# Causal masks added by VectorE in the instruction that finds the maximum, and the second gate's sums in the second layer

## The chip, the cores and the metric

The kernel runs on one core of one Trainium2 chip. Its engines work side by side: TensorE (PE in the profile, its weight loads PEld) multiplies, VectorE (DVE) and ScalarE (ACT) work element by element, GpSimd (POOL) prepares constants, SyncE (SP) issues most DMAs. The metric is the device time of one execution in microseconds; a lower time is better.

## The reference

Two layers work on x, 256 rows of 1024 numbers. Each normalises x, scales and shifts it by sums over `ada_w` (adaLN), mixes the rows by attention, and adds the result times a gate, which is another sum over `ada_w`. Layer 1 mixes with three attentions (compressed, selected and window keys), layer 2 with one; both have 16 heads of 64 that share 4 key heads. With 256 rows every window and every selection covers all earlier rows, so each score matrix has the same mask: a row sees the keys up to its own place.

```python
for i in range(DEPTH):
    shift, scale, gate = jnp.split(cond @ ada_w[i] + ada_b[i], 3, axis=-1)
    h = rms_norm(x, norm_g[i]) * (1 + scale[:, None, :]) + shift[:, None, :]
    ...
    x = x + gate[:, None, :] * y

def masked_softmax(s, mask):
    s = jnp.where(mask, s.astype(jnp.float32), -jnp.inf)
    m = jnp.max(s, axis=-1, keepdims=True)
    e = jnp.exp(s - jnp.where(jnp.isfinite(m), m, 0.0))
    return e / jnp.maximum(jnp.sum(e, axis=-1, keepdims=True), 1e-30)

p = masked_softmax(s_own, m_own).astype(v.dtype)
return jnp.einsum('bcgrk,bkgd->bcgrd', p, v_own)
...
return (o * jax.nn.silu(z)) @ w_out
```

## The kernel before

**The order of the work.** The program doesn't issue an instruction where the code calls it. `T`, `A`, `V`, `G`, `Q` record calls for TensorE, ScalarE, VectorE, GpSimd and SyncE in one `Plan`; at the end `plan.issue()` writes the order of each engine. It keeps a clock per engine, takes the cost of an instruction from `_cost`, the buffers of a tile from its tag, and among the operations that are ready the one that can start first, at equal times by a level: `URGENT`, `CHAIN`, `FILL`. So an operation recorded at `FILL` goes into gaps of the plan. All instructions carry line 373, the place in `issue()` that emits them; this document tells them apart by the names of their tiles. `_cost` gives a VectorE instruction 1.042 ns for each element and 68 ns (the line with `fast`), whether or not it also writes an accumulator.

**The products with weights.** A weight piece is 128 rows of 1024 numbers (512 KB), loaded by SP into `raw` (5 buffers). ScalarE rounds it into `hi` (4), VectorE subtracts, `lo = raw - hi` (4), and TensorE makes three products: hi with the high part of h, lo with the high part, hi with the low part. `chunk` does this for queries and keys; `z_blocks(w, c0, zT)` for the transposed z, in products of 256 columns at level `FILL`, into the two PSUM buffers `acc`; `out_products` for the output, with the transposed, gated heads in `qg`.

**The attention.** `make_q` normalises and rotates queries on VectorE (`ss`, `rs`, `n_out`, `rot`, `n_parts`), and TensorE transposes them. `scores` makes one PSUM tile `ps` for two heads: four products of 256 columns, and one more product of the identity in bf16 (`identB`) with a mask of 0 and a large negative number (`tri`, from `tri2`), which adds the mask. Then `top` finds the negative maximum of each row on VectorE (TENSOR_REDUCE into `tiny`), `exps` takes the exponential on ScalarE from PSUM into `p` (6 buffers) with the maximum as bias, and adds up the row. VectorE inverts the sums and scales `p`, TensorE transposes `p` (`ps<-identF,p`), ScalarE copies to `pT`, TensorE multiplies with the values (`ps<-pT,VA`), and VectorE multiplies with z (`g<-zT,ps`, then `qg<-g,qg`).

- `compressed(hf)`, twice in layer 1: scores of eight heads against 16 compressed keys, one mask product from `maskC` ahead of them, softmax in the tile `pc`, then its transposes (`ps<-identF,pc`).
- `pair_a(i)`, eight times in layer 1: three score groups for two heads (selected and window keys for the first 128 rows in one, then one each for the second 128 rows).
- `pair_b(i)`, eight times in layer 2: two score groups, 128 and 256 keys.

**Work in the background.** `side` is a list of generators, and `beside()` takes one step of the first of them. In layer 1 `beside()` is called between the pairs and the z pieces. The list holds the compression's products (`cmp_steps`), the first layer's gate (`ada_gate(0)`), and for the second layer two halves of scale and shift (`ada_ss`) with `ada_gate(1)` between them. `ada_gate(1)` loads eight pieces of `ada_w` into `raw` and sums them on VectorE, one SCALAR_TENSOR_TENSOR of 1024 elements each at level `FILL`; then two products with ones (`ps<-gate,ones`) spread the sum over the partitions. `x_update` of layer 2 needs that gate, behind the output products.

Of the kernel before, what the change touches and what calls it, by code (L numbers as in the profile page):

```python
# [9 lines left out]
F32 = mybir.dt.float32  # L10
# [7 lines left out]
P = 128  # L18
# [382 lines left out]
def kernel(  # L401
# [99 lines left out]

    identF = const.tile([P, P], F32, name="identF")
    make_identity(nc, identF)
    identB = const.tile([P, P], BF16, name="identB")
    make_identity(nc, identB)
# [19 lines left out]
    tri2 = const.tile([P, 2, P], BF16, name="tri2")  # L525
    nc.gpsimd.memset(tri2, 0.0)
    keep(tri2, [[0, 2], [-1, P]], 0)
    tri = tri2[:, 0, :]
    maskC = const.tile([P, 2, 8, 2, 16], BF16, name="maskC")
    nc.gpsimd.memset(maskC, 0.0)  # L530
    for m in range(2):
        keep(maskC[:, m, :, 0, :], [[0, 8], [-16, 16]], m * P - 31)
# [190 lines left out]
    def at_once(steps):  # L723
        for _ in steps:
            pass
# [128 lines left out]
        return [tile_of("qg", 4, S) for g in range(KVH)]  # L854


    def scores(q, kt, g, k0, n, heads, mk, at, need):

        s = tile_of("ps", 2, 256)
        with plan.group(need):  # L860
            for e in range(2):
                T.matmul(s[:, e, 0:n], q[heads[e]], kt[:, 0, g, k0:k0 + n], start=(e == 0), stop=False)
                T.matmul(s[:, e, 0:n], q[heads[e]], kt[:, 1, g, k0:k0 + n], start=False, stop=False)
            ms = s[:, :, at:at + mk.shape[1]]
            T.matmul(ms, identB, mk[:, None, :].to_broadcast([P, 2, mk.shape[1]]), start=False, stop=True)
        return s

    def top(dst, src):
        V.tensor_reduce(dst, src, axis=AX.X, op=OP.max, negate=True)

    def exps(dst, src, bias, total):
        A.activation(dst, src, AF.Exp, bias=bias, accum_out=total)

    def inverse(sm):
        V.tensor_scalar_max(sm, sm, 1e-30)
# [275 lines left out]
    def cmp_steps(hid):  # L1151

        for kq in range(4):
            for k in range(4):
                if k % 2 == 0:
                    w1 = [load(bass.AP(tensor=nsa_cmp_w1.tensor, offset=nsa_cmp_w1.offset + (kv * 2048 + kq * 512 + k * P) * 256,
                                       ap=[[256, P], [P * 256, 2], [1, 256]]), W1_HOME[kv]) for kv in range(2)]
                with plan.at(FILL), plan.group():
                    for kv in range(2):
                        T.matmul(hid[64 * kv:64 * kv + 64, 0:256],  # L1160
                                 FLAT[kv][kq // 2][:, 4 * (kq % 2) + k].rearrange("p g n -> p (g n)"), w1[kv][:, k % 2, :],
                                 start=(kq == 0 and k == 0), stop=(kq == 3 and k == 3), tile_position=(0, 64 * kv))
# [93 lines left out]
    def compressed(hf):  # L1256

        s = tile_of("ps", 2, 8, 2, 16)
        pc = tile_of("pc", 2, 8, 16)
        with plan.group(pc):  # L1260
            T.matmul(s.rearrange("p m h a n -> p (m h a n)"), identB, maskC.rearrange("p m h a n -> p (m h a n)"),
                     start=True, stop=False)
            for m in range(2):
                for h in range(8):
                    g = 2 * hf + h // 4
                    T.matmul(s[:, m, h], QT[g][:, h % 4, m * P:(m + 1) * P], KTA[:, :, g, 512:528],
                             start=False, stop=(m == 1 and h == 7))
# [12 lines left out]
        with plan.group():  # L1280
            for m in range(2):
                T.transpose(t[:, m * P:(m + 1) * P], pc[:, m].rearrange("p h n -> p (h n)"), identF)
        pcT[hf] = tile_of("pcT", S)
        A.copy(pcT[hf], t[:, 0:S])

    def pair_a(i):
        g, hf, j_ = i // 2, i // 4, i % 4
        ps = []
        neg, sm = tile_of("tiny", 2, 2, 2), tile_of("tiny", 2, 2, 2)
        for m, r, k0, mk, at in ((0, None, 128, tri2.rearrange("p r k -> p (r k)"), 0), (1, 1, 256, tri, P), (1, 0, 0, tri, 0)):  # L1290
            q = [QT[g][:, 2 * (i % 2) + e, m * P:(m + 1) * P] for e in range(2)]
            nb = 2 - m
            rs = slice(0, 2) if m == 0 else slice(r, 1 + r)
            p = tile_of("p", 2, nb, 256 // nb)
            s = scores(q, KTA, g, k0, 256, (0, 1), mk, at, p).rearrange("p e (r k) -> p e r k", r=nb)
            top(neg[:, m, :, rs], s)
            for e in range(2):
                for b in range(nb):
                    j = b if m == 0 else r
                    exps(p[:, e, b], s[:, e, b], neg[:, m, e, j:j + 1], sm[:, m, e, j:j + 1])  # L1300
            ps.append(p)
        smf = sm.rearrange("p m e r -> p (m e r)")
        V.reciprocal(smf, smf)
        for m in range(2):
            V.scalar_tensor_tensor(sm[:, m], sm[:, m], 1e30, gates[:, m, 2 * i:2 * i + 2, 1:3], op0=OP.min, op1=OP.mult)
        V.tensor_mul(ps[0], ps[0], sm[:, 0, :, :, None].to_broadcast([P, 2, 2, P]))
        for r in (1, 0):
            p = ps[2 - r]
            for e in range(2):
                V.tensor_scalar_mul(p[:, e, 0], p[:, e, 0], sm[:, 1, e, r:r + 1])  # L1310
        p0, p1 = ps[0], (ps[2], ps[1])
        pT = []
        for r in (1, 0):
            def block(e, b):
                if b == 0:
                    return p0[:, e, r]
                k = (b - 1) if r == 1 else (2 - b)
                return p1[r][:, e, 0, k * P:(k + 1) * P]

# [101 lines left out]
    raw_q = tile_of("n_in", 2, 512)  # L1421
    chunk(m_in, ((512, 512),), raw_part(raw_q, 512))
    make_q(raw_q, 4, QT, 2)
    zT = []
    for c0 in (1536, 2048):
        at_once(z_blocks(m_in, c0, zT))

    def pair_b(i):
        g = i // 2
        pm = [tile_of("p", 2, P), tile_of("p", 2, 256)]  # L1430
        neg, sm = tile_of("tiny", 2, 2), tile_of("tiny", 2, 2)
        for m in range(2):
            n = P * (m + 1)
            q = [QT[g][:, 2 * (i % 2) + e, m * P:(m + 1) * P] for e in range(2)]
            s = scores(q, KTB, g, 0, 256, (0, 1), tri, m * P, pm[m])
# [12 lines left out]

    for i in range(8):
        pair_b(i)  # L1450

    def done_b(m, sl, acc):
        x_update(1, m, sl, acc)
# [33 lines left out]
```

## Time and profile before

| what | us |
|---|---|
| median of 3 runs | 326.96 |
| fastest, slowest run | 326.69, 327.68 |
| profiled execution, first to last instruction (span) | 326.3 |
| profiled execution, its own time | not listed apart from its span |
| VectorE's first reduction of scores in layer 1 starts | 104.53 |
| VectorE's first reduction for the keys of layer 2 starts | 232.75 |
| last output product of layer 2 starts | 322.36 |

The busy shares, the chain and the stretches stand in the prediction. In a timeline row the columns are the start in us, the duration, the engine, the operation, out<-in with partitions × elements, and the count; idle time ahead of the row and what ended it stand in brackets at its end. A duration can reach past the start of the next instruction of the same engine, since they overlap; so what one instruction costs its engine is read from start to start.

### The profile page before, as it was taken

Reading aid. Unit: us, or ns where it says so; the run is one execution under the profiler, and the core shown is the slowest. Engines: PE = TensorE matmul, PEld = TensorE weight load, DVE = VectorE, ACT = ScalarE, POOL = GpSimd, SP = SyncE. Lnnn points to the kernel's source line nnn. Section 1 sums busy time; section 2 is a strip of 40 time slices with the busy share of each in tenths; the row PEclk is TensorE's granted clock in tenths of the full one; section 3 lists DMA queues with packets and bytes.
Section 4 is the critical chain, followed back from the end, with each engine's and each line's share of the span. In section 5 each row is a group of like instructions: output and inputs, shape, how many; then the busy total and the mean of one; then the engine's idle time right before and its main releaser. Section 6 shows DMA issues by size and latency. Waiting matters only on the chain.

```text
span 326.3 us, 6109 instructions
## 1 busy us (share of the span) xinstructions
PE 314.7 (96%) x2182; PEld 249.0 (76%) x2183; DVE 239.7 (73%) x580; ACT 202.5 (62%) x486; POOL 26.0 (8%) x98
## 2 busy tenths in 40 slices
PE   4899999999999999999999999998999999999995
PEld 4665677777657898679886588866888998988884
DVE  4753375669954999459998665997599899965754
ACT  5635246776536975558776675696675898965420
POOL 7038930000000000000000000000000000000000
PEclk9999999999999999999999999999999999999999
DMA  7999999559898605585267797627376513033102
GB/s 248 307 295 369 367 358 291 172 174 326 274 351 288 231 1 175 213 325 192 66 194 253 233 341 270 203 66 231 91 255 189 157 38 131 0 125 99 38 32 96
DMA packets 43994, 65.80 MB, mean 202 GB/s; under 512 B 4042, under 2 KB 20793, under 8 KB 43964
## 3 DMA queue, kind: packets, MB, share of 16 engines
q1 hardware_dynamic: 43796, 65.36, 60.6%
q8 instruction: 17, 0.28, 0.3%
q14 instruction: 13, 0.11, 0.1%
q10 hardware_dynamic: 168, 0.06, 0.1%
HBM read 64.36 MB, written 1.05 MB: 200 GB/s over the span
## 4 chain that ended last, share of the span: by engine, by line
PE 87%; DMA 4%; DVE 3%; ACT 3%; issue 1%; SPq 0%; ACTq 0%; DVEq 0%
PE ps L373 51%; PE acc L373 36%; DMA early<-in_ada_w_dram 2%; DMA raw<-in_nsa_w_in_dram 2%; ACT hi L373 1%; DVE lo L373 1%; ACT n_in L373 1%; DVE rs L373 1%; DMA rot<-in_c_dram 0%; ACT n_out L373 0%; ACT p L373 0%; DVE HT L373 0%; DVE p L373 0%; DVE y L373 0%; DVE X L373 0%
## 5 line engine op out<-in xcount | busy, mean ns | idle before, releaser
L373 DVE TENSOR_TENSOR lo<-raw,hi 128x1024 fp32r<-128x1024 f32 (+1 forms) x50 | 59.1, 1186 | 26.5 <-ACT hi L373 26.2
L373 ACT CAST hi<-raw 128x1024 fp32r<-128x1024 f32 (+1 forms) x50 | 51.0, 1026 | 32.7 <-PE acc L373 19.5
L373 PE MATMUL acc<-hi,HT 128*128 128x512 f32 (+1 forms) x176 | 54.6, 381 | 1.5 <-ACT HT L373 1.2
L373 PE MATMUL acc<-HT,hi 128*128 128x256 f32 x256 | 50.6, 289 | 0.0
L373 ACT ACTIVATE p<-ps,tiny 128x128 f32<-128x128 f32 (+1 forms) x96 | 39.6, 433 | 9.6 <-DVE tiny L373 9.3
L373 PEld LDWEIGHTS acc<-HT,hi 128*128 128x128 f32 x256 | 40.3, 189 | 0.9 <-issue 0.6
L373 PEld LDWEIGHTS acc<-hi,HT 128*128 128x128 f32 x176 | 32.0, 188 | 10.0 <-issue 2.4
L373 PE MATMUL acc<-HT,lo 128*128 128x256 f32 x128 | 36.9, 289 | 0.0
L373 PE MATMUL acc<-lo,HT 128*128 128x512 f32 (+1 forms) x88 | 33.5, 382 | 0.2 <-DVE lo L373 0.2
L373 PE MATMUL ps<-KTA,qg 128*128 128x256 f32 (+1 forms) x192 | 30.8, 297 | 0.0
L373 PE MATMUL ps<-hi,HT 128*128 128x512 f32 (+1 forms) x96 | 28.2, 367 | 0.0
L373 PEld LDWEIGHTS ps<-KTA,qg 128*128 128x128 f32 x192 | 26.0, 190 | 2.2 <-ACT p L373 1.0
L373 DVE TENSOR_REDUCE tiny<-ps 128x2 f32<-128x512 f32 (+2 forms) x40 | 24.9, 631 | 3.2 <-PE ps L373 2.8
L373 ACT COPY pT<-ps 128x384 f32<-128x384 f32 x48 | 20.9, 488 | 8.6 <-PE ps L373 8.3
L373 PEld LDWEIGHTS acc<-HT,lo 128*128 128x128 f32 x128 | 24.3, 190 | 0.5 <-issue 0.4
L373 PE MATMUL ps<-hi,qg 128*128 128x256 f32 (+1 forms) x96 | 23.6, 320 | 0.0
L373 PE MATMUL acc<-hi,qg 128*128 128x512 f32 x64 | 22.2, 397 | 0.0
L373 ACT ACTIVATION_READ_ACCUMULATOR p<-ps,tiny 128x1 f32 x96 | 20.8, 216 | 0.0
L373 PE MATMUL ps<-identF,p 128*128 128x128 f32 x144 | 20.7, 274 | 0.0
L373 PEld LDWEIGHTS ps<-hi,HT 128*128 128x128 f32 x96 | 16.8, 188 | 4.5 <-issue 2.5
L373 PEld LDWEIGHTS acc<-lo,HT 128*128 128x128 f32 x88 | 16.5, 188 | 3.6 <-DVE lo L373 1.2
L373 PE MATMUL ps<-pT,VA 128*64 128x256 f32 (+1 forms) x192 | 18.9, 334 | 0.0
(203 smaller groups left out, 576.1 us busy)
## 6 DMA issues: line engine op xcount, KB each, us to landing
raw<-in_ada_w_dram SPq DMA_DIRECT2D x32, 512.0 KB, 5.7
raw<-in_moba_w_in_dram SPq DMA_DIRECT2D x20, 512.0 KB, 4.1
early<-in_ada_w_dram SPq DMA_DIRECT2D x12, 512.0 KB, 9.7
raw<-in_nsa_w_in_dram SPq DMA_DIRECT2D x12, 512.0 KB, 6.4
early<-in_nsa_w_in_dram SPq DMA_DIRECT2D x9, 512.0 KB
p<-in_nsa_cmp_w_dram SPq DMA_DIRECT2D x16, 256.0 KB, 4.2
raw<-in_nsa_w_out_dram SPq DMA_DIRECT2D x8, 512.0 KB, 5.7
raw<-in_moba_w_out_dram SPq DMA_DIRECT2D x8, 512.0 KB, 4.2
```

Of the source, the lines that this page charges most:

```text
L373: r = getattr(self.engines[e], method)(*[self._real(a) for a in args], **{k: self._real(a) for k, a in kw.items()})
```

## The change

`identB`, `tri2` and the wide bf16 `maskC` go. A new constant `causal` of 384 columns holds zeros, the triangle and zeros; a window of it, 128 or 256 wide, is the mask of a score tile whose triangle begins at `at`. `scores` makes only its four products. `masked_top` is one VectorE instruction for each head's tile of 128 or 256 columns: it reads the scores from PSUM and the mask from SBUF, adds them, multiplies by −1, writes the negative masked scores to `p`, and gives their minimum as `neg`. The order lists it as two instructions, `ISA p,tiny<-ps,causal` and `ISA tiny 128x1`, the read of the accumulator. `exps` then works in `p`, with a scale of −1. There are 48 of 128 columns and 48 of 256, in place of 40 TENSOR_REDUCE; 42 mask products go (32 of 256 columns, 10 of 512). In `compressed` the mask product goes, and a copy becomes an addition of a small f32 mask. `ada_gate(1)` leaves the list of layer 1; it joins the list of layer 2 behind `make_q`, and its steps are taken between the z pieces and behind each `pair_b`.

```diff
-    side += [cmp_steps(hid), ada_gate(0), ada_ss(1, 0, 4), ada_gate(1), ada_ss(1, 4, 4)]
+    side += [cmp_steps(hid), ada_gate(0), ada_ss(1, 0, 4), ada_ss(1, 4, 4)]
...
-            ms = s[:, :, at:at + mk.shape[1]]
-            T.matmul(ms, identB, mk[:, None, :].to_broadcast([P, 2, mk.shape[1]]), start=False, stop=True)
...
+    def masked_top(dst, src, neg, at):
+
+        mask = causal[:, P - at:P - at + src.shape[-1]]
+        V.tensor_tensor_reduce(dst, src, mask, -1.0, 3.0e38, op0=OP.add, op1=OP.min, accum_out=neg)
+
+    def exps(dst, bias, total):
+        A.activation(dst, dst, AF.Exp, bias=bias, scale=-1.0, accum_out=total)
...
-            T.matmul(s.rearrange("p m h a n -> p (m h a n)"), identB, maskC.rearrange("p m h a n -> p (m h a n)"),
-                     start=True, stop=False)
...
-        V.tensor_copy(pc, s[:, :, :, 1])
+        V.tensor_add(pc, s[:, :, :, 1], maskC[:, :, None, :].to_broadcast([P, 2, 8, 16]))
...
-            top(neg[:, m, :, rs], s)
             for e in range(2):
                 for b in range(nb):
                     j = b if m == 0 else r
-                    exps(p[:, e, b], s[:, e, b], neg[:, m, e, j:j + 1], sm[:, m, e, j:j + 1])
+                    masked_top(p[:, e, b], s[:, e, b], neg[:, m, e, j:j + 1], at)
...
     make_q(raw_q, 4, QT, 2)
+    side.append(ada_gate(1))
     zT = []
     for c0 in (1536, 2048):
-        at_once(z_blocks(m_in, c0, zT))
+        for _ in z_blocks(m_in, c0, zT):
+            beside()
...
-            top(neg[:, m], s[:, :, 0:n])
             for e in range(2):
-                exps(pm[m][:, e], s[:, e, 0:n], neg[:, m, e:e + 1], sm[:, m, e:e + 1])
+                masked_top(pm[m][:, e], s[:, e, 0:n], neg[:, m, e:e + 1], m * P)
+            for e in range(2):
+                exps(pm[m][:, e], neg[:, m, e:e + 1], sm[:, m, e:e + 1])
...
     for i in range(8):
         pair_b(i)
+        beside()
```

What the planner makes of it is shown at three places. Up to the first scores the orders of before and of the change agree; numbers behind a name count tiles and differ between the two.

VectorE at the first pair of heads of layer 1, where `rs` is the second query norm, before:

```order
L373 TENSOR_REDUCE tiny_1141<-ps_201 128x4
L373 TENSOR_SCALAR rs_177<-ss_170 128x16
L373 TENSOR_REDUCE tiny_1141<-ps_167 128x2
L373 TENSOR_SCALAR rs_177<-rs_177 128x16
L373 TENSOR_TENSOR rs_177<-rs_177 128x16 x2
```

and of the change:

```order
L373 ISA p_712,tiny_1136<-ps_196,causal 128x128
L373 ISA tiny_1136 128x1
L373 TENSOR_SCALAR rs_172<-ss_165 128x16
L373 ISA p_712,tiny_1136<-ps_196,causal 128x128
L373 ISA tiny_1136 128x1
L373 TENSOR_SCALAR rs_172<-rs_172 128x16
L373 ISA p_712,tiny_1136<-ps_196,causal 128x128
L373 ISA tiny_1136 128x1
L373 TENSOR_TENSOR rs_172<-rs_172 128x16
L373 ISA p_712,tiny_1136<-ps_196,causal 128x128
L373 ISA tiny_1136 128x1
```

One reduction of a group has become four masked maxima with four reads; all three pairs of heads that VectorE works on ahead of the transposes of the first `pc` have them. On TensorE seven more z products and four more products with `condz` stand ahead of those transposes.

VectorE at the last pair of heads of layer 2 (`p_719`, `p_723` before, `p_714`, `p_718` in the change), before:

```order
L373 TENSOR_SCALAR tiny_1175<-tiny_1175 128x4
L373 RECIPROCAL tiny_1175<-tiny_1175 128x4
L373 TENSOR_SCALAR p_719<-p_719,tiny_1175 128x128 x2
L373 TENSOR_SCALAR p_723<-p_723,tiny_1175 128x256 x2
L373 TENSOR_TENSOR lo_373<-raw_654,hi_358 128x1024
L373 TENSOR_TENSOR lo_264<-raw_645,hi_252 128x1024
L373 SCALAR_TENSOR_TENSOR zT_729<-y_238,acc_313 128x512
L373 SCALAR_TENSOR_TENSOR zT_742<-y_148,acc_280 128x512
```

and of the change:

```order
L373 SCALAR_TENSOR_TENSOR gate_181<-raw_640,condz,gate_181 128x1024
...
L373 TENSOR_TENSOR lo_348<-raw_618,hi_334 128x1024
L373 SCALAR_TENSOR_TENSOR zT_724<-y_143,acc_308 128x512
L373 TENSOR_SCALAR p_714<-p_714,tiny_1140 128x128
L373 SCALAR_TENSOR_TENSOR g_1154<-zT_724,ps_156 128x256
L373 SCALAR_TENSOR_TENSOR g_1190<-zT_724,ps_196 128x256
L373 TENSOR_SCALAR p_714<-p_714,tiny_1140 128x128
L373 SCALAR_TENSOR_TENSOR zT_737<-y_233,acc_275 128x512
L373 TENSOR_TENSOR qg_1565<-g_1154,qg_1565 128x256
L373 TENSOR_TENSOR qg_1565<-g_1190,qg_1565 128x256
L373 SCALAR_TENSOR_TENSOR g_1154<-zT_737,ps_219 128x256
L373 TENSOR_SCALAR p_718<-p_718,tiny_1140 128x256 x2
```

The last two z tiles and five operations that use them now stand ahead of the last scaling. The row at the top is the last of the eight gate sums; the other seven stand ahead of it, the first behind the key rotation of layer 2 (`n_out<-n_in,TC`). The number of `lo` rows ahead of the last scaling is the same in both.

TensorE just ahead of the last pair's transposes, before:

```order
L373 MATMUL ps_161<-pT_1310,VA 64x256
L373 MATMUL ps_161<-pT_1280,VA 64x256
L373 MATMUL ps_161<-pT_1310,VA 64x128
L373 MATMUL ps_161<-pT_1280,VA 64x128
L373 MATMUL ps_167<-identF,p_719 128x128
L373 MATMUL ps_167<-identF,p_723 128x128 x2
...
L373 MATMUL acc_280<-HT,hi_358 128x256
```

and of the change:

```order
L373 MATMUL ps_238<-gate_181,ones 128x512
...
L373 MATMUL ps_211<-gate_181,ones 128x512
L373 MATMUL acc_308<-hi_334,qg_1448 128x512
L373 MATMUL acc_308<-lo_348,qg_1448 128x512
L373 MATMUL acc_308<-hi_334,qg_1448 128x512 x2
L373 MATMUL acc_308<-lo_348,qg_1448 128x512
L373 MATMUL ps_162<-identF,p_714 128x128
L373 MATMUL ps_162<-identF,p_718 128x128 x2
```

Before, z products stood behind the last transposes, as the last row shows; now the z products, the two spreading products and five output products all stand ahead of them, and only output products and this pair's own follow.

More of the change, by code (lines that the diff above doesn't have):

```diff
@@ L503 @@
     make_identity(nc, identF)
-    identB = const.tile([P, P], BF16, name="identB")
-    make_identity(nc, identB)
     condz = const.tile([P, 8, 32], F32, name="condz")
@@ L523, in keep @@
                                 compare_op=OP.is_ge, fill=MASKED)
[L525 to L529, printed above, removed]
+    causal = const.tile([P, 3 * P], BF16, name="causal")
+    nc.gpsimd.memset(causal, 0.0)
+    keep(causal[:, P:2 * P], [[-1, P]], 0)
+    maskC = const.tile([P, 2, 16], F32, name="maskC")
     nc.gpsimd.memset(maskC, 0.0)
     for m in range(2):
-        keep(maskC[:, m, :, 0, :], [[0, 8], [-16, 16]], m * P - 31)
+        keep(maskC[:, m, :], [[-16, 16]], m * P - 31)
     selG = const.tile([P, 2, P], F32, name="selG")
@@ L854, in qt_tiles, with scores @@
         return [tile_of("qg", 4, S) for g in range(KVH)]
-    def scores(q, kt, g, k0, n, heads, mk, at, need):
+    def scores(q, kt, g, k0, n, need):
         s = tile_of("ps", 2, 256)
@@ L861, in scores @@
             for e in range(2):
-                T.matmul(s[:, e, 0:n], q[heads[e]], kt[:, 0, g, k0:k0 + n], start=(e == 0), stop=False)
-                T.matmul(s[:, e, 0:n], q[heads[e]], kt[:, 1, g, k0:k0 + n], start=False, stop=False)
-            ms = s[:, :, at:at + mk.shape[1]]
-            T.matmul(ms, identB, mk[:, None, :].to_broadcast([P, 2, mk.shape[1]]), start=False, stop=True)
+                T.matmul(s[:, e, 0:n], q[e], kt[:, 0, g, k0:k0 + n], start=(e == 0), stop=False)
+                T.matmul(s[:, e, 0:n], q[e], kt[:, 1, g, k0:k0 + n], start=False, stop=(e == 1))
         return s
@@ L1266, in compressed @@
                     T.matmul(s[:, m, h], QT[g][:, h % 4, m * P:(m + 1) * P], KTA[:, :, g, 512:528],
-                             start=False, stop=(m == 1 and h == 7))
+                             start=(m == 0 and h == 0), stop=(m == 1 and h == 7))
         neg, sm = tile_of("tiny", 2, 8), tile_of("tiny", 2, 8)
-        V.tensor_copy(pc, s[:, :, :, 1])
+        V.tensor_add(pc, s[:, :, :, 1], maskC[:, :, None, :].to_broadcast([P, 2, 8, 16]))
         V.tensor_add(pc, s[:, :, :, 0], pc)
@@ L1289, in pair_a @@
         neg, sm = tile_of("tiny", 2, 2, 2), tile_of("tiny", 2, 2, 2)
-        for m, r, k0, mk, at in ((0, None, 128, tri2.rearrange("p r k -> p (r k)"), 0), (1, 1, 256, tri, P), (1, 0, 0, tri, 0)):
+        for m, r, k0, at in ((0, None, 128, 0), (1, 1, 256, P), (1, 0, 0, 0)):
             q = [QT[g][:, 2 * (i % 2) + e, m * P:(m + 1) * P] for e in range(2)]
             nb = 2 - m
-            rs = slice(0, 2) if m == 0 else slice(r, 1 + r)
             p = tile_of("p", 2, nb, 256 // nb)
-            s = scores(q, KTA, g, k0, 256, (0, 1), mk, at, p).rearrange("p e (r k) -> p e r k", r=nb)
-            top(neg[:, m, :, rs], s)
+            s = scores(q, KTA, g, k0, 256, p).rearrange("p e (r k) -> p e r k", r=nb)
             for e in range(2):
@@ L1299, in pair_a @@
                     j = b if m == 0 else r
-                    exps(p[:, e, b], s[:, e, b], neg[:, m, e, j:j + 1], sm[:, m, e, j:j + 1])
+                    masked_top(p[:, e, b], s[:, e, b], neg[:, m, e, j:j + 1], at)
+            for e in range(2):
+                for b in range(nb):
+                    j = b if m == 0 else r
+                    exps(p[:, e, b], neg[:, m, e, j:j + 1], sm[:, m, e, j:j + 1])
             ps.append(p)
@@ L1434, in pair_b @@
             q = [QT[g][:, 2 * (i % 2) + e, m * P:(m + 1) * P] for e in range(2)]
-            s = scores(q, KTB, g, 0, 256, (0, 1), tri, m * P, pm[m])
-            top(neg[:, m], s[:, :, 0:n])
+            s = scores(q, KTB, g, 0, 256, pm[m])
             for e in range(2):
-                exps(pm[m][:, e], s[:, e, 0:n], neg[:, m, e:e + 1], sm[:, m, e:e + 1])
+                masked_top(pm[m][:, e], s[:, e, 0:n], neg[:, m, e:e + 1], m * P)
+            for e in range(2):
+                exps(pm[m][:, e], neg[:, m, e:e + 1], sm[:, m, e:e + 1])
         inverse(sm.rearrange("p m e -> p (m e)"))
@@ L1450 @@
         pair_b(i)
+        beside()
+    assert not side
     def done_b(m, sl, acc):
```

2 lines of the change are left out of this document (removed).

## The prediction

> **What bounds the kernel now.** I read the page's busy shares and its chain first, because they say which engine a saving must come from.
>
> ```profile
> span 326.3 us, 6109 instructions
> PE 314.7 (96%) x2182; PEld 249.0 (76%) x2183; DVE 239.7 (73%) x580; ACT 202.5 (62%) x486; POOL 26.0 (8%) x98
> PE 87%; DMA 4%; DVE 3%; ACT 3%; issue 1%; SPq 0%; ACTq 0%; DVEq 0%
> ```
>
> TensorE is busy 96% of the span and makes 87% of the chain, so a product taken away should shorten the run. VectorE's 73% looks like room, but it is an average over stages. So the stretches come next; the columns are busy time, then clock, DMA share and GB/s.
>
> ```profile
> core 0: us, PE busy (x) PEld busy (x) DVE busy (x) ACT busy (x) POOL busy (x), PEclk, DMA share, GB/s
> 137.00:192.00 55.00, 54.92 (x450) 41.80 (x447) 43.45 (x100) 39.86 (x128) 0.00 (x0) 1.00 0.64 214
> 231.00:258.00 27.00, 27.00 (x150) 23.11 (x148) 25.32 (x51) 18.76 (x27) 0.00 (x0) 1.00 0.62 190
> 258.00:292.00 34.00, 34.00 (x300) 30.59 (x300) 30.87 (x96) 30.00 (x98) 0.00 (x0) 1.00 0.20 68
> 292.00:326.00 34.00, 30.64 (x191) 26.41 (x187) 18.42 (x28) 10.44 (x15) 0.00 (x0) 1.00 0.22 77
> ```
>
> The middle of layer 1 leaves VectorE 11.6 us idle out of 55. The second layer's attention (231 to 292) leaves it 61.00 − 25.32 − 30.87 = 4.8 us out of 61. The change puts work into both, but most of it into the full one. The granted clock is 1.00 throughout and plays no part.
>
> **What goes: the mask products.** TensorE's timeline around the first scores of layer 2 prices them (start, duration, what).
>
> ```profile
> 259.33 0.71 PE L373 MATMUL ps<-KTA,qg 128*128 128x256 f32 x4
> 259.88 0.28 PE L373 MATMUL ps<-tri,identB 128*128 128x256 bf16 x1
> 259.92 0.71 PE L373 MATMUL ps<-KTA,qg 128*128 128x256 f32 x4
> ...
> 267.52 0.64 PE L373 MATMUL ps<-KTA,qg 128*128 128x256 f32 x4
> 268.00 0.28 PE L373 MATMUL ps<-tri,identB 128*128 128x256 bf16 x1
> ...
> 299.95 0.39 PE L373 MATMUL ps<-hi,qg 128*128 128x512 f32 x1
> 300.19 0.39 PE L373 MATMUL ps<-lo,qg 128*128 128x512 f32 x1
> ```
>
> A group with its mask takes 259.92 − 259.33 = 0.59 us, the four products alone 268.00 − 267.52 = 0.48, so a mask of 256 columns is worth about 0.12. One of 512 columns is taken as the 512-column step of the last two rows, 0.24. Layer 1 loses 16 × 0.12 + 10 × 0.24 (eight for window and selection, two for the compressed scores) = 4.3 us, layer 2 loses 16 × 0.12 = 1.9.
>
> **What comes: VectorE's masked maxima.** One reduction over a score group becomes two or four fused operations, each with an accumulator read behind it, which no row of the profile shows. VectorE's starts, not its durations, price them, since the next one starts before the last has ended.
>
> ```profile
> 122.17 0.28 DVE L373 TENSOR_TENSOR rot<-n_out,TS 128x128 f32<-128x128 f32 x1
> 122.37 0.27 DVE L373 TENSOR_TENSOR n_parts<-kcy,n_parts 64x128 fp32r<-64x128 f32 x1
> ...
> 147.69 0.42 DVE L373 TENSOR_TENSOR qg<-g,qg 128x256 fp32r<-128x256 f32 x1
> 148.03 1.28 DVE L373 TENSOR_REDUCE tiny<-ps 128x2 f32<-128x512 f32 x2
> 149.23 1.28 DVE L373 SCALAR_TENSOR_TENSOR gate<-raw,condz,gate 128x1024 f32<-128x1024 f32 x1
> 150.42 0.42 DVE L373 COPY pc<-ps 128x256 f32<-128x256 f32 x1
> ...
> 260.07 0.37 ACT L373 ACTIVATE p<-ps,tiny 128x128 f32<-128x128 f32 x1
> 260.33 0.19 ACT L373 ACTIVATION_READ_ACCUMULATOR p<-ps,tiny 128x1 f32 x1
> 260.43 0.36 ACT L373 ACTIVATE p<-ps,tiny 128x128 f32<-128x128 f32 x1
> ```
>
> From start to start: 0.20 for 128 elements with two inputs, 0.34 for 256, 0.60 for one 512-wide reduction (two in 1.20), 1.19 for one gate sum. The nearest row for the unknown read is ScalarE's own: it starts at 260.33 and the next operation at 260.43, 0.10 later. Rows of small VectorE work bound it.
>
> ```profile
> 106.43 0.18 DVE L373 SCALAR_TENSOR_TENSOR rs<-rs 128x16 f32<-128x16 f32 x1
> 106.64 0.38 DVE L373 TENSOR_TENSOR rs<-rs 128x16 f32<-128x16 f32 x2
> 107.67 0.16 DVE L373 TENSOR_TENSOR tiny<-ps,RT 128x4 f32<-128x4 f32 x1 [0.65 <-PE ps L373]
> 107.74 0.17 DVE L373 SCALAR_TENSOR_TENSOR rs<-rs 128x16 f32<-128x16 f32 x1
> ```
>
> A small operation that waits for its forerunner costs 0.21 (106.43 to 106.64), one that doesn't 0.07 (107.67 to 107.74). I take ScalarE's **0.10**, the only read of the same kind, and keep 0 and 0.21 as ends: one instruction more can't give time back, so nothing lies below 0. The Trainium skill's page "VectorE: DVE Perf Modes", section "Two Vector instructions with no wait between them", says that such an operation is two instructions, and that each is held back only for tiles that start in another group of partitions; all here start at partition 0, so by that rule the read isn't held and costs what the 0.07 row costs. No row here shows the read itself.
>
> So a 128-wide masked maximum is 0.30 and a 256-wide one 0.44. A pair of heads in layer 1 has four of each, 2.96, for three reductions of 0.60: +1.16 us. A pair in layer 2 has two of each, 1.48, for one reduction of 512 (0.60) and one of 256 (0.34): +0.54.
>
> ScalarE's exponentials read SBUF instead of PSUM.
>
> ```profile
> L373 ACT CAST qg<-g 128x256 fp32r<-128x256 f32 x16 | 6.3, 412 | 4.3 <-DVE g L373 4.2
> L373 ACT COPY n_in<-ps 128x256 f32<-128x256 f32 x4 | 1.5, 368 | 0.0
> ```
>
> These rows put 0.044 us on that (412 − 368 ns), 32 × 0.044 = 1.4 us in layer 2, where ScalarE has 4 of 34 idle: hidden there, and on the path at worst. Adding the small mask in the compressed scores replaces a copy of as many elements: nothing.
>
> **Layer 1.** It loses 4.3 us of mask products, eight gate sums on VectorE (8 × 1.19 = 9.5 us) and the two products that spread the gate over the partitions.
>
> ```profile
> 107.67:134.17 26.50, 26.50 (x218) 22.76 (x217) 25.82 (x89) 19.32 (x62) 0.00 (x0) 1.00 0.39 129
> ...
> 131.18 0.69 DVE L373 SCALAR_TENSOR_TENSOR zT<-y,acc 128x512 f32<-128x512 f32 x1 [0.58 <-ACT y L373]
> 133.75 0.42 DVE L373 TENSOR_TENSOR pc<-pc,tiny 128x256 f32<-128x256 f32 x1
> 137.77 0.42 DVE L373 SCALAR_TENSOR_TENSOR g<-zT,ps 128x256 f32<-128x256 f32 x1 [3.60 <-PE ps L373]
> ...
> 134.64 0.38 PE L373 MATMUL ps<-identF,pc 128*128 128x128 f32 x2
> ...
> 178.05 1.02 PE L373 MATMUL ps<-gate,ones 128*128 128x512 f32 x2
> 178.91 0.49 PE L373 MATMUL ps<-identF,p 128*128 128x128 f32 x3
> 179.33 1.06 PE L373 MATMUL ps<-raw,condz 128*32 128x512 f32 x8
> ```
>
> One spreading product (two instructions) runs 178.05 to 178.91, 0.86; two make 1.7. Against this: from 107.67 to 134.17 VectorE is busy 25.82 of 26.50 us, and three pairs' masked maxima stand there, 3 × 1.16 = 3.5 us more. Less the holes of 0.65 (107.67) and 0.58 (131.18), the compressed probabilities are ready at 136.4 instead of 134.17. TensorE reached their transposes at 134.64. Ten masks ahead of them go (six of 0.12, four of 0.24: 1.7), and by the order seven z products (a step of 0.12, as for the four products of 256 columns above) and four products with condz (1.06 / 8 = 0.13) move ahead of them: 1.3. It would be there at 134.2 and waits **2.2 us**. Behind that VectorE idled 3.60 us and then has the gate sums less, so I expect no second wait. Layer 1: −4.3 − 1.7 + 2.2 = **−3.8 us**.
>
> **Layer 2.** The eight gate sums land between the first key rows and the last pair's scaling, as VectorE's rows in the section on the change show. By the order, seven operations that fold in the second half of z (two zT of 512, three g and two qg of 256) also stand ahead of that scaling now: 2 × 0.60 + 5 × 0.34 = 2.9 (prices of the same widths above). VectorE's added work is 8 × 1.19 + 8 × 0.54 + 2.9 = **16.7 us**. I let 3.6 of the 4.8 idle us absorb it (an engine in order doesn't fill each gap), with 0 and 4.8 as ends (3.6 us worse, 1.2 better): 13.1 us later.
>
> ```profile
> 291.13 1.01 DVE L373 TENSOR_SCALAR p<-p,tiny 128x128 f32<-128x128 f32 x4
> ...
> raw<-in_moba_w_in_dram SPq DMA_DIRECT2D x20, 512.0 KB, 4.1
> ```
>
> The last scaling ended at 292.14 and would end at 305.2. Who waits? TensorE had z products until 299.95, which covered the old end. It now has everything ahead of the last pair's transposes done at 299.95 − 1.9 (masks) + 1.7 (spreading products) + 1.2 (five output products, 5 × 0.24, now ahead) − 1.0 (the last pair's transposes and value products, which were ahead and are behind; six and four instructions, by the 0.49 of three transposes above) = 300.0, and **waits 5.2 us**. The stage ends 5.2 − 1.9 + 1.7 = **5.0 us** later. The cover is the point of the whole case: VectorE may come 300.0 − 292.1 = 7.9 us later than before without a wait, and comes 13.1 later.
>
> The gate's eight DMAs of 512 KB go past other weight pieces in SP's queue and take five raw buffers in turn. DMA share is 0.62, then 0.20 in this stage; they fit, and I cost them at nothing. If that cover were gone, one piece late is one landing, the 4.1 us of the last row.
>
> Behind the wait stand the same output products as before, with their weight pieces' subtractions paced as before (18.42 busy of 34), so the end moves by as much as their start.
>
> **Sum.** −3.8 + 5.0 = +1.2 us on the profiled span of 326.3, so 327.5. The 0.66 us between that span and the median of 326.96 (the page gives no other time for this execution) lie around it and stay: **328.2 us**.
>
> **The rivals.** First, *TensorE stays the bound and the change is faster*. If the read costs nothing, VectorE's debt in layer 2 is 16.7 − 32 × 0.10 = 13.5; less 3.6 it comes 9.9 late, TensorE waits 2.0, and layer 2 ends 1.8 later. In layer 1 the 24 reads take 2.4 with them and with that the wait: −6.0. Net −4.2: **322.8 us**. For it speaks the 96% of TensorE; against it, that no VectorE operation in these rows is free. Per 0.01 of the read the net moves by 0.32 + 0.24 us, so it decides below about 0.06.
>
> Second, *the read is cheap and the layers cancel*: at the 0.07 of the row that waits for nothing, layer 1 gives −4.5 and layer 2 costs 4.0: **326.5 us**, within 0.3%, which is about what a measurement of this kernel can tell from no change.
>
> Third, *each read waits for the operation ahead of it*, as the rs row does: 0.11 more is +3.5 in layer 2 and +2.6 in layer 1, net +7.3: **334.3 us**. For it: the read needs the result of the operation right ahead. Against: ScalarE's read doesn't show it. The reductions from 148.03 end at 149.31 and the next row starts at 149.23, so VectorE does start an operation before the last has ended. By the same page's section "The DRAIN you can't avoid", an operation starts only when the pipe of the one ahead is empty, unless it isn't held; by that rule a held read would cost its whole duration, by ScalarE's row 0.19, and the time would be near this rival's. The trace agrees only with the exception.
>
> Fourth, *the gate's DMAs delay a weight piece*: one landing, **332.3 us**. Against it stands the low DMA share.
>
> **How the numbers follow.** Forecast (a read of 0.09 to 0.15, or VectorE's idle time filled less well): 0.40. First rival 0.25, second 0.23, third 0.09, fourth 0.03. Slower by over 0.3%: 0.40 + 0.09 + 0.03 = 0.52; same 0.23; faster 0.25. The range of 8 in 10 takes in the first rival's time and stops short of the third's, with about a tenth left out at either side: 322.7 to 333.0. The forecast's own part of it is 327.9 to 331, by reads of 0.10 to 0.15.
>
> **What would show it.** In the changed profile: masked maxima of 256 starting 0.44 apart with their read (the read's own row is the first thing to look at); TensorE idle about 2 us near 134 to 137, released by VectorE or the compressed probabilities; VectorE over 95% busy from 231 to 300; TensorE idle about 5 us ahead of the last pair's transposes. The forecast is wrong if VectorE has idle time in layer 2, if TensorE does not wait ahead of those transposes, or if the wait's releaser is a DMA.

## The result, and the profile after

| kernel | median us | lowest to highest | span of the profiled execution |
|---|---|---|---|
| before | 326.82 (4 runs) | 326.59 to 327.68 | 326.3 |
| the change | 322.16 (4 runs) | 321.59 to 322.42 | 320.5 |

The ratio is 0.9849, with an interval of 0.9819 to 0.9879: the change is 1.5% faster. The forecast was 328.2; the time lies just below the range of 322.7 to 333.0, and close to the first rival's 322.8. Here the profiled execution's own time is known too, 322.3 beside its span of 320.5: 1.8 us lie around the span, not the 0.66 that the prediction took. Before's other executions have 1.7 us around the span, so its profiled one (326.3) was some 1 us longer than its median. The spans differ by 5.8 us, the medians by 4.7: up to 1 us of a difference between two profiles can belong to the executions and not to the change. Ratios and intervals go by fast runs alone: one run of before (331.79), one of `loads_and_sums` (331.93) and one of `change_third` (699.36) are left out.

The page of the change, busy shares and chain:

```profile
span 320.5 us, 6156 instructions
PE 307.2 (96%) x2141; PEld 245.3 (77%) x2141; DVE 242.1 (76%) x732; ACT 204.9 (64%) x486; POOL 24.8 (8%) x96
PE 72%; DVE 12%; DMA 7%; ACT 4%; issue 3%; ACTq 0%; SPq 0%; DVEq 0%
```

TensorE is busy 7.5 us less and still 96% of the span, so the end followed it. VectorE is busy only 2.4 us more. Its share of the chain went from 3% to 12%: it now ends more waits.

The same stretches (the last one ends with the span; each lies a little later in the program, since the kernel runs ahead):

```profile
137.00:192.00 55.00, 55.00 (x455) 45.04 (x452) 42.08 (x164) 43.71 (x131) 0.00 (x0) 1.00 0.53 175
...
231.00:258.00 27.00, 27.00 (x180) 24.43 (x179) 26.55 (x52) 18.64 (x25) 0.00 (x0) 1.00 0.79 257
258.00:292.00 34.00, 33.03 (x281) 29.01 (x280) 33.76 (x143) 31.02 (x99) 0.00 (x0) 1.00 0.34 110
```

VectorE is as full in layer 2 as forecast, 60.3 of 61 us. VectorE's timeline of the change at the first pair shows what that work costs (start, duration):

```profile
104.34 0.28 DVE L373 CUSTOM_DVE_ANT_0 p<-ps,causal 128x128 f32<-128x128 f32 x1
104.55 0.08 DVE L373 DVE_READ_ACCUMULATOR2_ANT tiny<- 128x1 f32 x1
104.55 0.17 DVE L373 TENSOR_SCALAR rs<-ss 128x16 f32<-128x16 f32 x1
104.62 0.28 DVE L373 CUSTOM_DVE_ANT_0 p<-ps,causal 128x128 f32<-128x128 f32 x1
...
105.50 0.42 DVE L373 CUSTOM_DVE_ANT_0 p<-ps,causal 128x256 f32<-128x256 f32 x1
105.85 0.08 DVE L373 DVE_READ_ACCUMULATOR2_ANT tiny<- 128x1 f32 x1
105.85 0.17 DVE L373 SCALAR_TENSOR_TENSOR rs<-rs 128x16 f32<-128x16 f32 x1
```

A masked maximum of 128 takes 0.21 to what follows, one of 256 takes 0.35, as forecast. But the read starts at 104.55 and so does the next operation: **the read takes no time of VectorE that shows**, where the prediction put 0.10. Of the 96 reads, 87 start in the same hundredth of a microsecond as the operation behind them. The masked maxima also stand between `rs` operations that wait for each other, 0.20 apart in before's rows; here such an operation takes 0.07 (104.55 to 104.62), and a masked maximum fills the rest.

To compare the layers I take the span apart at two rows of TensorE's timeline: its first score products of layer 1 (`ps<-KTA,qg`, 103.62 before, 103.34 after) and the first product of layer 2 (`acc<-KTA,HT`, 214.98 and 207.48). The same is done for each run below.

| us | before | change | difference | forecast |
|---|---|---|---|---|
| layer 1, from its first scores | 111.36 | 104.14 | −7.2 | −3.8 |
| layer 2, to the end of the span | 111.29 | 112.98 | +1.7 | +5.0 |

The change's two other profiled executions (`change_again`, `change_third`) give 104.22 and 104.12, and 113.08 and 113.03.

TensorE's waits in layer 2 of the change, and the rows of the places that the prediction named:

```profile
134.26 0.38 PE L373 MATMUL ps<-identF,pc 128*128 128x128 f32 x2
...
211.25 0.51 PE L373 MATMUL acc<-lo,HT 128*128 128x512 f32 x1 [0.57 <-DVE lo L373]
...
213.60 1.39 PE L373 MATMUL ps<-identF,n_in 128*128 128x128 f32 x8 [0.45 <-DVE n_in L373]
...
216.82 0.50 PE L373 MATMUL acc<-lo,HT 128*128 128x512 f32 x1 [0.66 <-DVE lo L373]
...
218.82 0.50 PE L373 MATMUL acc<-KTA,HT 128*128 128x512 f32 x1 [0.35 <-ACT VA L373]
...
262.18 0.39 PE L373 MATMUL acc<-HT,hi 128*128 128x256 f32 x1 [0.97 <-DVE zT L373]
...
293.72 0.82 PE L373 MATMUL ps<-identF,p 128*128 128x128 f32 x6
```

Neither the transposes of the compressed probabilities (134.26) nor the last pair's (293.72) have a wait in brackets. VectorE's rows show when it had done, for the first `pc` and for the last scaling:

```profile
133.25 0.42 DVE L373 TENSOR_TENSOR pc<-pc,tiny 128x256 f32<-128x256 f32 x1
...
293.10 0.61 DVE L373 TENSOR_SCALAR p<-p,tiny 128x256 f32<-128x256 f32 x2
```

The last scaling ended at 293.71, so there the two engines came together. What TensorE waits for instead is the layer's boundary, 2.03 us in four pieces where before had one of 1.03, and the first zT, 0.97: VectorE has to empty the `acc` buffers before the second half of z can begin. The four pieces at the boundary stand in `before_no_gate` (1.98 us) and `after_no_gate` (2.02) too, which have no gate sums for layer 2 at all, and `loads_added`, which has them where the change has them, waits 1.02 like before. So neither the masks nor the sums in layer 2 make them; why the planner's order does in some kernels wasn't followed.

### The profile page after: what moved, and what is told of

Read it like the earlier page. It is cut to its first block, busy times and chain, and to the rows that moved or that the text cites. A ratio compares the mean times of both kernels' runs of the same rounds, so it can differ in the third digit from the quotient of the medians.

```text
span 320.5 us, 6156 instructions
## 1 busy us (share of the span) xinstructions
PE 307.2 (96%) x2141; PEld 245.3 (77%) x2141; DVE 242.1 (76%) x732; ACT 204.9 (64%) x486; POOL 24.8 (8%) x96
## 4 chain that ended last, share of the span: by engine, by line
PE 72%; DVE 12%; DMA 7%; ACT 4%; issue 3%; ACTq 0%; SPq 0%; DVEq 0%
PE ps L373 46%; PE acc L373 26%; DVE lo L373 3%; DVE rs L373 2%; DMA p<-in_nsa_cmp_w_dram 2%; DMA raw<-in_nsa_w_in_dram 2%; DMA y<-in_ada_b_dram 2%; ACT n_out L373 1%; DVE gate L373 1%; DVE n_out L373 1%; DMA early<-in_nsa_w_in_dram 1%; ACT hi L373 1%; ACT HT L373 1%; DVE p L373 1%; DVE ss L373 1%
## 5 line engine op out<-in xcount | busy, mean ns | idle before, releaser
L373 PE MATMUL acc<-HT,hi 128*128 128x256 f32 x256 | 49.8, 285 | 1.0 <-DVE zT L373 1.0
L373 ACT ACTIVATE p<-p,tiny 128x128 f32<-128x128 f32 (+1 forms) x96 | 42.9, 454 | 7.5 <-DVE tiny L373 7.4
L373 DVE CUSTOM_DVE_ANT_0 p<-ps,causal 128x128 f32<-128x128 f32 (+1 forms) x96 | 30.9, 346 | 3.3 <-PE ps L373 3.3
L373 PE MATMUL ps<-KTA,qg 128*128 128x256 f32 (+1 forms) x192 | 27.1, 286 | 0.0
L373 ACT COPY pT<-ps 128x384 f32<-128x384 f32 x48 | 21.7, 483 | 5.7 <-PE ps L373 5.6
L373 PEld LDWEIGHTS ps<-KTA,qg 128*128 128x128 f32 x192 | 24.1, 189 | 1.6 <-issue 1.4
L373 PE MATMUL ps<-identF,p 128*128 128x128 f32 x144 | 21.7, 277 | 0.0
L373 PEld LDWEIGHTS ps<-identF,p 128*128 128x128 f32 x144 | 16.1, 141 | 3.5 <-issue 1.0
```

Source lines behind the costliest of these rows:

```text
L373: r = getattr(self.engines[e], method)(*[self._real(a) for a in args], **{k: self._real(a) for k, a in kw.items()})
```

## The experiments

Ratios are to before on the same chip, with their intervals in the text where they decide.

**The price of the read.** `read_as_forecast` puts the forecast's price behind every read:

```diff
-        V.tensor_tensor_reduce(dst, src, mask, -1.0, 3.0e38, op0=OP.add, op1=OP.min, accum_out=neg)
+        with plan.group() as op:
+            V.tensor_tensor_reduce(dst, src, mask, -1.0, 3.0e38, op0=OP.add, op1=OP.min, accum_out=neg)
+            op["calls"].append(("tensor_copy", (spare, identF[:, 0:64]), {}))
```

> The changed kernel with a copy of 128x64 on VectorE behind each of the 96 accumulator reads, in an otherwise unchanged order: about 0.10 us each, the price that the prediction gave to the read; the copies go nowhere. Theory 1 (only the price of the read was wrong): TensorE waits about 2 us for the first compressed probabilities and about 5 us ahead of the last pair's transposes, 327.5 to 329, as the prediction had it (328.2). Theory 2 (TensorE's cover was counted too small as well): the same 9.6 us on VectorE cost less, 323 to 326.

329.14 us, a ratio of 1.0059 (1.0029 to 1.0089). Its VectorE rows:

```profile
105.14 0.42 DVE L373 CUSTOM_DVE_ANT_0 p<-ps,causal 128x256 f32<-128x256 f32 x1
105.48 0.09 DVE L373 DVE_READ_ACCUMULATOR2_ANT tiny<- 128x1 f32 x1
105.48 0.20 DVE L373 COPY spare<-identF 128x64 f32<-128x64 f32 x1
105.58 0.17 DVE L373 SCALAR_TENSOR_TENSOR rs<-rs 128x16 f32<-128x16 f32 x1
```

The copy takes 0.10, as meant. With it the change is slower than before, by about what was forecast (+0.6% measured, +0.4% forecast). Layer 1 takes 107.82 (−3.5 on before; forecast −3.8), layer 2 116.93 (+5.6; forecast +5.0). So the sums came out right for their price, but not by the waits that they were made of, and that is luck: here too no wait stands at the compressed probabilities (their transposes start at 135.58 without one). Layer 1 lost its time in many small waits, the largest part that was found at the transposes of `p` (from start to start they sum to some 1.3 us more than in the change), and layer 2 lost 1.83 us at the first zT, after which the clock fell in this execution (see the last section).

**Who brought the gain: masks or gate?** Two runs do one half of the change each. `gate_layer1` keeps the masks on VectorE and puts the gate back:

```diff
-    side += [cmp_steps(hid), ada_gate(0), ada_ss(1, 0, 4), ada_ss(1, 4, 4)]
+    side += [cmp_steps(hid), ada_gate(0), ada_ss(1, 0, 4), ada_gate(1), ada_ss(1, 4, 4)]
...
-    side.append(ada_gate(1))
```

> The changed kernel with the second gate's sums and spreading products back in layer 1, masks by VectorE as in the change. Theory 1 (the masks bring the gain, the moved sums cost a little in layer 2): VectorE has 9.5 us less in layer 2, TensorE's wait of 0.97 us for zT near 262 goes, layer 1 takes the sums in the 12.9 us that VectorE idled there: 321 to 322.5, same as the change (322.2) or up to 1 us faster. Theory 2 (the moved sums made room in layer 1 for the masked maxima): VectorE is at 51.6 of 55 us between 137 and 192, TensorE waits 2 to 3 us there: 324 to 326.

`gate_moved_only` is before with the gate's lines of the change (the list, the `append`, and `beside()` between z pieces and behind each pair).

> The kernel of before with only the second gate's sums moved to layer 2, masks by products. Theory 1: layer 1 loses two spreading products (1.7 us), layer 2 gets them and VectorE comes 8.8 us later to the last scaling, which TensorE's work just covers: 326 to 328, no change against before (326.8). Theory 2 (the move itself is a good part of the gain): 323 to 325.

| kernel | us | ratio | layer 1 | layer 2 |
|---|---|---|---|---|
| before | | 1 | 111.36 | 111.29 |
| masks only (`gate_layer1`) | 326.16 | 0.9976 (0.9954 to 0.9999) | 112.74 | 108.87 |
| gate only (`gate_moved_only`) | 331.26 | 1.0123 (1.0091 to 1.0156) | 109.15 | 117.49 |
| both (the change) | 322.16 | 0.9849 (0.9819 to 0.9879) | 104.14 | 112.98 |

Theory 1 falls. Theory 2 comes near in one run only: `gate_layer1` lies just above its 324 to 326, and TensorE idles 2.6 of the 55 us between 137 and 192 there, but VectorE is busy 44.95 of them and not 51.6. `gate_moved_only` is outside both. (Of its layer 2, 2.57 us are a wait at the first zT and 1.7 a lower clock behind it.) The masks alone bring 0.2%, the gate's move alone costs 1.2%, and together they bring 1.5%. The surplus is in layer 1, where the masks alone add 1.4 us, the move alone takes 2.2 away, and both take 7.2. What holds layer 1 with the gate in it is seen in ScalarE's and TensorE's rows of `gate_layer1`:

```profile
188.43 1.04 ACT L373 CAST hi<-raw 128x1024 fp32r<-128x1024 f32 x1 [2.39 <-DMA raw<-in_nsa_w_out_dram]
...
191.98 1.05 ACT L373 CAST hi<-raw 128x1024 fp32r<-128x1024 f32 x1 [0.68 <-DMA raw<-in_nsa_w_out_dram]
194.86 1.05 ACT L373 CAST hi<-raw 128x1024 fp32r<-128x1024 f32 x1 [1.83 <-DMA raw<-in_nsa_w_out_dram]
```

```profile
189.53 0.50 PE L373 MATMUL acc<-hi,qg 128*128 128x512 f32 x1 [1.33 <-ACT hi L373]
```

The output weights land late: six of the eight are waited for. In before ScalarE waits for none of them. SP's rows tell when the first of them was issued, in before and in the change (before's view ends at 192, ahead of the last two):

```profile
180.90 8.79 SPq L373 DMA_DIRECT2D raw<-in_nsa_w_out_dram  x6
```

```profile
159.54 21.46 SPq L373 DMA_DIRECT2D raw<-in_nsa_w_out_dram  x8
```

With the gate's loads gone from SP's queue ahead of them, they go out 21 us earlier. In `gate_layer1` the first goes out at 182.01. The first output product of layer 1 in before, in `gate_moved_only` (weights out from 160.0, no wait for one) and in the change:

```profile
189.42 0.48 PE L373 MATMUL acc<-hi,qg 128*128 128x512 f32 x1
```

```profile
189.29 0.39 PE L373 MATMUL acc<-hi,qg 128*128 128x512 f32 x1
```

```profile
184.11 0.50 PE L373 MATMUL acc<-hi,qg 128*128 128x512 f32 x1
```

With the row of `gate_layer1` above (189.53), three of the four kernels reach it at the same time, and the change comes five us earlier. So TensorE and the weights both held layer 1 at nearly the same time, and either edit alone left the other in place. The output weights are not all of it: layer 1 of `gate_layer1` is 8.6 us longer than the change's, of which 2.0 are the spreading products, some 3.5 waits that TensorE's rows show, and the rest short pauses, among them at `ps<-raw,condz`, which takes its pieces straight from `raw` (11.2 us from start to start, 8.7 in the change).

**Loads or sums?** Theory 3 said loads. `loads_added` and `sums_added` each put one half of the gate's work back into layer 1 of the change, in addition to the gate in layer 2; `loads_and_sums` puts both. Their edits, in this order:

```diff
+        for kk in range(8):
+            w = ada_piece(1, kk, 2 * D, D)[:, 0, :]
+            with plan.at(FILL):
+                V.tensor_copy(spare[:, kk:kk + 1], w[:, 0:1])
+            yield
...
+            with plan.at(FILL), plan.group(after=[len(plan.ops) - 1]):
+                for _ in range(4):
+                    V.scalar_tensor_tensor(spare, spare, condz[:, kk, 0:1], spare, op0=OP.mult, op1=OP.add)
...
+            with plan.at(FILL):
+                V.scalar_tensor_tensor(w, w, condz[:, kk, 0:1], w, op0=OP.mult, op1=OP.add)
```

> The changed kernel with eight more loads of 512 KB in layer 1, at the place where the second gate's loads were before (the same pieces of ada_w into raw; VectorE reads one column of each, and nothing uses it). Theory 3 (with the mask products gone, layer 1 is bound by its weight loads, and the change gains there because the gate's 4 MB moved out): ScalarE waits for output weights, TensorE waits 2 to 4 us more before the layer's end: 324.5 to 326.5. Theory 2 (it was VectorE's room for the sums): under 0.7 us more than the change: 322 to 323.

> The changed kernel with eight more groups of VectorE work in layer 1 (four operations of 224 columns, about 1.2 us each group, in a scratch tile that nothing uses), without loads. Theory 3 (loads bind layer 1): VectorE's idle 12.9 us between 137 and 192 take them: 322 to 323. Theory 2 (the sums on VectorE bind): TensorE waits 2 to 4 us more in layer 1: 324.5 to 326.5.

> The changed kernel with both: eight more loads in layer 1 and on each loaded piece one VectorE operation of 1024 elements, in place in its raw buffer (nothing uses the result). It keeps the raw buffer until VectorE comes, as the gate's sums in layer 1 did. Loads alone cost 1.5 us over the change, sums alone 2.0. If the two are independent: 325 to 326.5, a ratio near 0.995. If the buffers that wait for VectorE make it worse (layer 1 took 7 us longer with the real gate there, beside its spreading products): 327 to 329.5, a ratio of 1.000 to 1.006.

With `change_again` (322.32, ratio 0.9854) beside them, loads cost 1.5 us (323.78) and sums 2.0 (324.29): each between the two ranges that had been expected, so both have a part. Together they cost more than the sum: 326.77, a ratio of 1.0007 (0.9976 to 1.0037) against the change's 0.985, about 5 us (the time lies between its two expected ranges, the ratio in the second). Layer 1 took 106.14, 107.12 and 109.56. The first output weight went out at 177.8, 157.6 and 178.4. A piece that waits for VectorE keeps one of the five raw buffers, which fits the surplus, but the buffers were not tried by themselves.

> The change itself, beside the others on the same chip: 322.2, a ratio of 0.985 to before.

**The masks without any gate.** In `before_no_gate` and `after_no_gate` the second gate is a tile of ones; its loads, sums and spreading products are left out.

```diff
         if l:
-            G.memset(gate, 0.0)
-            Q.dma_start(gate[0:1], bias)
+            G.memset(gate, 1.0)
+            return
```

> The kernel of before without the second layer's gate (its eight loads, sums and two spreading products are left out, and the gate is 1). Theory 3 (in layer 1 the output weights stand in SP's queue behind the gate's loads; the masks' products are TensorE's own time): layer 1 about 2 us shorter by the spreading products, layer 2 as before: 324 to 325.5, a ratio of 0.990 to 0.996.

> The change without the second layer's gate (left out in the same way). Theory 3: layer 1 as in the change (207.5), layer 2 as in the run with the gate in layer 1 (108.9): 318 us, a ratio of 0.970 to 0.976, so that the masks alone are worth 6 to 7 us where no gate loads are in their way, against 0.8 us with the gate in layer 1. Rival (masks and gate act independently of each other): the masks are worth 0.8 us here too: 323.5 to 324.5.

326.59 (ratio 0.9964) and 319.88 (0.9759): the masks are worth 6.7 us where no gate is in the way, as theory 3 had it, against 0.2% with the gate in layer 1. In layer 1 `after_no_gate` takes 104.14, exactly what the change takes; its layer 2 takes 110.1 where 108.9 was expected, and the time is 1.9 us above the 318 expected. In `before_no_gate` the output weights go out early, at 160.0, and layer 1 still takes 109.11: with the masks on TensorE, early weights alone don't help. `before_no_gate` came a little above what was expected; its layer 2 is 1.1 us longer than before's, and 0.95 of that is the wait at the layer's boundary in four pieces, 1.98 in place of 1.03. The gate costs the change 2.4 us (322.3 − 319.9).

**The masks of layer 2.** `masks_layer1_only` has the masks of `pair_b` by products again.

```diff
+            if at is not None:
+                tri = causal[:, P:2 * P]
+                T.matmul(s[:, :, at:at + P], identB, tri[:, None, :].to_broadcast([P, 2, P]), start=False, stop=True)
...
+            top(neg[:, m], s[:, :, 0:n])
...
-                masked_top(pm[m][:, e], s[:, e, 0:n], neg[:, m, e:e + 1], m * P)
```

> The changed kernel with the masks of layer 2 by products again (16 products of 256 columns, and TENSOR_REDUCE for the maxima), layer 1 as in the change. Theory 1: layer 2 gets back 1.9 us of mask products, VectorE has 16 x 0.21 + 16 x 0.35 - 8 x 0.94 = 1.4 us less there, which TensorE didn't wait for: 323.5 to 324.5. Theory 2 (VectorE's load in layer 2 costs as much as the products): 322, same as the change.

326.77, a ratio of 0.9983 (0.9957 to 1.0008), a worse miss than either theory: layer 2 takes 116.75, 3.8 more than in the change. Of that, 1.9 are the products as forecast, and 1.6 a longer wait at the first zT (2.57 us instead of 0.97): VectorE gets the zT two us later, behind whole reductions and one more `lo`, in the order that the planner makes of it. So in this order VectorE's masks in layer 2 pay twice, although the layer leaves VectorE little room. The profiled execution (325.41) is the fastest of twelve; by their ratios the median is 4.4 us above the change's, and the last section says what the others show.

**Where to put the gate.** Three runs try other places. `gate_later` calls `beside()` only from the second z block on; `gate_pool` gives the sums to GpSimd; `gate_halves` does four pieces in layer 1 and four in layer 2:

```diff
-    side += [cmp_steps(hid), ada_gate(0), ada_ss(1, 0, 4), ada_ss(1, 4, 4)]
+    second = ada_gate(1)
+    side += [cmp_steps(hid), ada_gate(0), ada_ss(1, 0, 4), islice(second, 4), ada_ss(1, 4, 4)]
...
-    side.append(ada_gate(1))
+    side.append(second)
```

> The changed kernel with the gate's steps in layer 2 beginning one z block later (with the second block, then behind each pair). Theory 1 (two gate sums right ahead of the first zT make TensorE wait 0.97 us at 262): that wait goes and 321.0 to 321.8 is left. Rival: the sums that come later now stand ahead of the last pair's scaling, where VectorE already came at the same moment as TensorE (293.71 and 293.72), and each costs its 1.2 us there: 323 to 325.

> The change with the gate's sums on GpSimd (a product and a sum for each piece, in the place of VectorE's one operation), in layer 2 as in the change. Theory 1 (VectorE's 9.5 us for the gate cost TensorE 1 us at the first zT and up to 3 us in all in layer 2): 319 to 321.5, a ratio of 0.975 to 0.982. Rival (GpSimd is slower on a piece and keeps its raw buffer longer, or slows VectorE's accesses): weight pieces come late in layer 2, 323 to 327.

> The change with the first four of the gate's pieces in layer 1 and the last four and the spreading in layer 2. If layer 1 has room for half (its loads and VectorE's 12.9 idle us between 137 and 192): layer 1 under 0.5 us longer, the wait of 0.97 us at the first zT of layer 2 gone: 321 to 322, a ratio of 0.980 to 0.984. If each piece costs in layer 1 what it cost in the run with the whole gate there (7 us for eight): 324 to 326.

> The change itself beside the others on the same chip: a ratio of 0.985 to before.

`gate_later`: 323.16, at the lower edge of its rival's range, ratio 0.9864 beside 0.9854 of `change_again`; no gain. The wait at the first zT only shrank to 0.75, and the spreading products, now behind late sums, wait 0.39. `gate_pool`: 342.81, the rival's side and far beyond it (last section). **`gate_halves`: 320.80, ratio 0.9798 (0.9767 to 0.9830) beside 0.9850 (0.9807 to 0.9893) of `change_third`: 1.0 us less, with every one of its six runs (320.0 to 321.03) below all of that run's (from 321.63).** That is a little better than the 321 to 322 expected. Layer 1 has room for half: it takes 104.07. In layer 2 TensorE's rows of `gate_halves` show where the microsecond went (its file is one line longer, hence L374):

```profile
260.08 0.28 PE L374 MATMUL acc<-HT,hi 128*128 128x256 f32 x1
260.20 1.88 PE L374 MATMUL ps<-gate,ones 128*128 128x512 f32 x4
261.51 0.68 PE L374 MATMUL acc<-HT,hi 128*128 128x256 f32 x1
```

The gate is complete earlier, so its spreading products fill the hole in which TensorE waited for zT. `gate_halves` is the fastest of the kernels that compute the whole reference.

## Why the prediction was wrong

- **The read.** "I take ScalarE's 0.10, the only read of the same kind": this term was mis-sized. It measured 0.00, and it carried the sign: with 0 the same working gives the first rival, 322.8, 0.6 us from the result. A row of another engine had been preferred. The Trainium skill's page "VectorE: DVE Perf Modes", section "Two Vector instructions with no wait between them", pointed the right way: by its rule the read isn't held here, and the trace agrees (104.55 and 104.55).
- **Mask products and spreading.** The prices hold roughly. For the 24 score masks of layer 1 they give 3.8 us; the rows sum to 2.3 from start to start, and the score products beside them are 0.8 shorter in all, 3.1. The masks of 512 columns were put too high: 0.13 by their own rows, not 0.24. Layer 2 gained 1.75 (1.9 forecast). The two spreading products left layer 1 with 1.8 (1.7) and cost 1.5 in layer 2. That is 4.9 of the 7.2 that layer 1 lost; the rest are short pauses that went, the largest at `ps<-pcT,Vbd` (1.0 us from start to start) and at `ps<-raw,condz` (0.75).
- **The wait of 2.2 us at the compressed probabilities.** It doesn't exist, with the read at 0 or at 0.10. The step that failed is "VectorE is busy 25.82 of 26.50 us", read as no room. Part of that busy time was `rs` operations waiting for each other, and the masked maxima went into it: the probabilities came 30.3 us after the first scores, against 30.6 before.
- **Layer 1's saving as TensorE's own.** −4.3 − 1.7 was put down without asking what else held the layer. It came near (−7.2 against the first rival's −6.0) because the same change took the gate's loads, and its sums, out of layer 1, and for that the prediction had no term beyond the spreading products: it is luck. The prediction counted the loads where they arrive, in layer 2, at nothing, which held, and not where they leave; with the gate left in layer 1 the masks bring 0.2%.
- **Layer 2.** VectorE's room was judged rightly (60.3 of 61 us busy). The wait ahead of the last pair, 5.2 us in the forecast and 2.0 with a read of 0, didn't come: TensorE came there at the moment VectorE had done. It had waited earlier: 0.97 at the first zT, which must free an `acc` buffer before more z products can run, and 1.0 more than in before at the boundary, which the sums in layer 2 don't make. +1.7 came where the first rival had worked out +1.8, by other waits, and so by luck.
- **The fourth rival** (a late weight piece in layer 2) didn't come: none of TensorE's waits in the change behind the first scores ends on a DMA.
- **Two smaller slips.** The time around the span was taken as 0.66 us and is 1.8. By the prediction's own 0.56 us for each 0.01 of the read, its part of 327.9 to 331 for reads of 0.10 to 0.15 begins at 328.2.

## What to carry to other kernels

Price an instruction that a trace doesn't show by its own engine's rows first, and when the sign hangs on that one price, let the chances say so. Before a saving on the busiest engine is put down in full, look for what would hold the stage next (here the output weights in the DMA queue), and count a moved transfer at the place it leaves as well as where it arrives. Two edits, of which one brings 0.2% and the other costs 1.2%, can bring 1.5% together when two resources hold a stage at the same time.

## What the hardware showed that I had not expected

The accumulator read of VectorE takes 81 ns by its own row and starts together with the operation behind it in 87 of 96 cases. In the other nine that operation starts 0.04 to 1.19 us later; three of these rows show a wait for another engine, and the rest weren't followed.

TensorE's granted clock fell after a wait of about 2 us. In `read_as_forecast` it waited 1.83 us up to 266.37, and then (TensorE's busy time, its clock, DMA share and GB/s):

```profile
266.00:267.00 1.00, 0.63 (x5) 1.00 0.06 25
267.00:268.00 1.00, 1.00 (x7) 0.50 0.01 4
...
269.00:270.00 1.00, 1.00 (x7) 0.50 0.00 0
270.00:271.00 1.00, 1.00 (x9) 0.80 0.00 0
271.00:272.00 1.00, 1.00 (x11) 1.00 0.00 0
```

Half the clock for some 3.4 us is 1.7 us lost on top of the wait. `gate_moved_only` shows the same after 2.57 us; `masks_layer1_only` waited 2.57 us at the same place and kept its clock in the profiled execution, so it doesn't follow each time. Its other executions fit this: four of the twelve have a mean clock of 1.00 and take 326.0 us on average, eight have 0.995 and take 327.3. Of `read_as_forecast`'s ten, six have 1.00 (328.8) and four 0.990 to 0.995 (330.2). After the change's 0.97 us the clock stayed at 1.00.

VectorE slowed down beside GpSimd. In `gate_pool` GpSimd was at the gate's sums from 234 to 282, and some of VectorE's rows became long there, like this subtraction, which takes 1.22 elsewhere; a reduction at 258.50 beside GpSimd took its usual 1.21. TensorE waited 8.38 us for VectorE, up to 260.36. What GpSimd lost isn't shown, since no run has these operations of GpSimd without VectorE at work:

```profile
254.88 3.36 DVE L373 TENSOR_TENSOR lo<-raw,hi 128x1024 fp32r<-128x1024 f32 x1
```

```profile
257.14 4.06 POOL L373 TENSOR_SCALAR raw<-raw,condz 128x1024 f32<-128x1024 f32 x1
```
